# A turned bank of q and k that only ScalarE reads

## The chip, the core and the metric

The kernel runs on one core of one Trainium2 chip. What counts is the device time of one execution in microseconds (us). The names of the engines are those of the profile: PE is TensorE, DVE VectorE, ACT ScalarE, POOL GpSimd, SP SyncE; SBUF is the on-chip memory, PSUM the eight banks into which PE writes its products and its transposes.

## The reference

One layer of a hybrid decoder over 1024 tokens of width 1024, all in float32. An input projection feeds three head groups side by side: a gated short convolution, eight heads of stick-breaking attention, and a spatial gate; then an output projection, a squared-ReLU MLP, and an embedding with a gate. The part that this change touches is the QK norm and the scores:

```python
q = rms_norm(q.reshape(bsz, s_len, ATTN_HEADS, HEAD_DIM), q_norm_g[i])
k = rms_norm(k.reshape(bsz, s_len, ATTN_HEADS, HEAD_DIM), k_norm_g[i])
...
z = jnp.einsum('bqhd,bkhd->bhqk', qi, kj) * scale
log_rem = jnp.where(causal, jax.nn.log_sigmoid(-z), 0.0)
suffix = lax.cumsum(log_rem, axis=3, reverse=True) - log_rem
weights = jnp.where(causal, jnp.exp(log_beta + suffix), 0.0)
```

## The kernel before

**Two parts for each number.** PE multiplies in a rounded format (fp32r). Each operand is therefore kept as a hi part (the value rounded by ScalarE as it copies) and a lo part (the value less its hi part, made by VectorE), and a product is three matmuls: hi by hi, hi by lo, lo by hi. `split` (L130 to L139) makes such a pair: ScalarE writes hi, VectorE subtracts.

**Stages.** First the projection of the embedding and the norm of x, then the gate's and the first pair's projections, then attention, then the output projection, the MLP (products by a Strassen-like scheme, L814), the last gate. The attention stage runs from about 85 to 410 us. It weaves two streams: `attention()` goes through four pairs of heads (`pr`), and `fill` carries the projections of the pairs 1 to 3 (`project`, L340) and then the convolution. `weave` (L284) takes pieces from both so that PE has projection matmuls to do while the attention of the pair before waits for other engines. The order in which instructions stand in each engine's queue is set when the kernel is built, by a scheduler that plays the program on a model of time; a changed instruction can thus move its neighbours.

**The projection of a pair.** For each block of 128 tokens, `project` collects q, k and v of two heads in a PSUM bank (`qkv_ps`). ScalarE squares q and k (L376), VectorE sums (`ss`, L379), GpSimd takes the power -1/2 (`rs`, L170), VectorE writes q and k times `rs` to the SBUF tile `qk` (L384; one tile holds two blocks, and there are two such tiles). ScalarE and VectorE make v's parts (`V`, L137 and L138), and only then the bank `qkv_ps` is free for the next block.

**The turn.** After two blocks, `turn_qk` (L394) lets PE transpose the tile: four transposes go into one bank, `qk_tr`, q of both blocks in columns 0 to 255 and k in 256 to 511. There are 16 such turns, four for each pair of heads. Of the bank, ScalarE writes q's hi part to `QS` (L137) and k's to `KH` (L407); VectorE makes q's lo part `low_q` (L138, `q_lo` in the profile) and, for each of the two heads, k's lo part on that head's 64 rows (`KL`, L409, twice). After every second turn, copies bring the two heads' rows to their places (L413 to L418). The framework that places the semaphores lets only one engine at a time at a PSUM bank, readers included. So the bank changes hands: ScalarE (QS), VectorE (q_lo), ScalarE (KH), VectorE (KL, KL).

**Attention.** `stick` multiplies QS by KH and KL (`z`, L448 and L450), ScalarE takes the sigmoid (`rem`, L452), VectorE scans backwards (L457), and the weights are differences of neighbours (`wt`, L464), on VectorE for three of eight row blocks, on GpSimd for the rest. `gather` transposes the weights (`w_tr`, L486), splits them (`wT_hi`, `wT_lo`), and multiplies by V (`av`, L504). The banks of `qk_tr` and `w_tr` come from one pool of three (`ps_tr`): as long as one of the three is not read out, the other two have to do.

Of the kernel before, what the change touches and what calls it, by code (L numbers as in the profile page):

```python
# [10 lines left out]
AF = mybir.ActivationFunctionType  # L11
ALU = mybir.AluOpType
# [21 lines left out]
def hybrid_block(ctx: ExitStack, tc: tile.TileContext, a: dict):  # L34
# [5 lines left out]
    nc = tc.nc  # L40
# [42 lines left out]
    def bank(pool, s):  # L83
        return pool.tile([P, HT], F32, tag=pool.name, name=name(s))
# [30 lines left out]
    def load_const(key, shape):  # L115
        t = const.tile(list(shape), F32, name=f"c_{key}")
        nc.gpsimd.dma_start(t, a[key])
        return t
# [6 lines left out]
    gq = load_const("gq", [P, 1])  # L125
# [5 lines left out]
    def split(src, hi, lo, scale=None, low=nc.vector):  # L131

        if scale is None:
            last_hi[0] = nc.scalar.copy(hi, src)  # L134
            low.tensor_tensor(out=lo, in0=src, in1=hi, op=ALU.subtract)  # L135
        else:
            nc.scalar.activation(hi, src, AF.Copy, scale=scale)  # L137
            nc.vector.scalar_tensor_tensor(out=lo, in0=src, scalar=scale, in1=hi,  # L138
                                           op0=ALU.mult, op1=ALU.subtract)  # L139
# [205 lines left out]
    def project(pr):  # L345
# [11 lines left out]
        for t in range(KT):  # L357
# [34 lines left out]
            if t % 2 == 1:  # L392
                later(72, lambda t=t, qk=qk: turn_qk(heads[pr], t, qk))

    def turn_qk(head, t, qk):

        QS, KH, KL, _, low_q = head
        th = t // 4
        tr = bank(ps_tr, "qk_tr")
        for i in range(2):  # L400
            for j in range(2):
                o = j * 256 + i * P
                nc.tensor.transpose(tr[:, o:o + P], qk[:, i, j * P:(j + 1) * P], ident)
        ws = slice((t % 4 - 1) * P, (t % 4 + 1) * P)

        split(tr[:, :256], QS[0][th][:, ws], low_q[th][:, ws], scale=gq)
        nc.scalar.activation(KH[0][th][:, ws], tr[:, 256:], AF.Copy, scale=gk)  # L407
        for hh, own in enumerate((lo_p, hi_p)):
            nc.vector.scalar_tensor_tensor(out=KL[hh][th][own, ws], in0=tr[own, 256:],  # L409
                                           scalar=gk[own], in1=KH[0][th][own, ws],  # L410
                                           op0=ALU.mult, op1=ALU.subtract)
        if t % 4 == 3:
            nc.scalar.copy(KH[1][th][hi_p], KH[0][th][hi_p])  # L413
            nc.scalar.copy(KH[1][th][lo_p], KH[0][th][hi_p])
            nc.scalar.copy(KH[0][th][hi_p], KH[0][th][lo_p])
            nc.vector.tensor_copy(QS[1][th][hi_p], QS[0][th][hi_p])
            nc.vector.tensor_copy(QS[1][th][lo_p], low_q[th][hi_p])
            nc.vector.tensor_copy(QS[0][th][hi_p], low_q[th][lo_p])  # L418
        return 8
# [331 lines left out]
    def late_slot(tag, s, dt=F32):  # L751
        return late.tile([P, HT], dt, tag=tag, name=name(s), bufs=LATE[tag])
# [172 lines left out]
    for h in range(2):  # L925
        for n in (0, 4, 1, 5, 2, 6, 3, 7):
# [28 lines left out]
            t = hg[n][h] = late_slot("tmp", "hg")  # L955
# [151 lines left out]
    def residual(n, h):  # L1107
        if h_res[n][h] is None:
            h_res[n][h] = slot("h")
            nc.sync.dma_start(h_res[n][h], h_dram[n, h])  # L1110
        return h_res[n][h]
# [28 lines left out]
    for s, (c, p, j) in enumerate(steps):  # L1140
# [13 lines left out]
        elif p == 6:  # L1154
            subtract(nc.vector, u_sum[j], u_sum[j], bank)
            if last:
                add(nc.vector, h_res[j][1], h_res[j][1], u_sum[j])
                for h in range(2):
                    t = residual(j + 4, h)
                    subtract(nc.vector, t, t, u_sum[j])  # L1160
        elif p in (2, 3):
            t = residual(j, p - 2)
# [3 lines left out]
        else:  # L1166
            h = 0 if p == 4 else 1
            t = residual(j + 4, h)
# [55 lines left out]
    for p in GATE:  # L1224
        for j in range(4):
# [14 lines left out]
            for bank, c in zip(banks, cs):  # L1240
# [8 lines left out]
                elif p == 5:  # L1249
                    e_of[j] = late_slot("tmp", "e")  # L1250
                    add(nc.vector, e_of[j], bank, v_of[j])
                    t = late_slot("tmp", "gt")
                    add(nc.vector, t, d_bank.pop((3, j))[0], e_of[j])
                    gated(j, 1, t, t, c, by_dma=True)
                elif p == 7:
                    t = e_of[j][:, c]
                    add(nc.vector, t, bank, t)
                    gated(j + 4, 1, t, t, c, -1.0, True)
                elif p == 4:
                    t = v_of[j][:, c]  # L1260
# [84 lines left out]
```

## Time and profile before

| | |
|---|---|
| median of 3 runs | 1207.3 us (1204.84 to 1210.0) |
| the profiled execution, its own time | 1206.75 us |
| its span, first to last instruction | 1205.0 us |
| PE busy | 1181.0 us, 98% |
| DVE busy | 885.7 us, 73% |
| ACT busy | 595.5 us, 49% |
| POOL busy | 400.5 us, 33% |
| granted PE clock | 0.997 |

The page of the profile first gives busy times by engine. Its chain of waits goes back from the last instruction to what released each step. The view of waits tells, for each engine, which instruction stood idle and what ended it. The table by stretches gives the busy time of each engine in a part of the span, so that PE's idle time can be laid to a stage. The view of groups gives the number of instructions of one line and shape and the mean duration of one.

### The profile page before, as it was taken

Reading aid. Unit: us, or ns where it says so; the run is one execution under the profiler, and the core shown is the slowest. Engines: PE = TensorE matmul, PEld = TensorE weight load, DVE = VectorE, ACT = ScalarE, POOL = GpSimd, SP = SyncE. Lnnn points to the kernel's source line nnn. Section 1 sums busy time; section 2 is a strip of 40 time slices with the busy share of each in tenths; the row PEclk is TensorE's granted clock in tenths of the full one; section 3 lists DMA queues with packets and bytes.
Section 4 is the critical chain, followed back from the end, with each engine's and each line's share of the span. In section 5 each row is a group of like instructions: output and inputs, shape, how many; then the busy total and the mean of one; then the engine's idle time right before and its main releaser. Section 6 shows DMA issues by size and latency. Waiting matters only on the chain.

```text
span 1205.0 us, 17538 instructions
## 1 busy us (share of the span) xinstructions
PE 1181.0 (98%) x5788; PEld 1007.1 (84%) x5788; DVE 885.7 (73%) x1310; ACT 595.5 (49%) x1148; POOL 400.5 (33%) x472
## 2 busy tenths in 40 slices
PE   9999899998999999999999999999999999999997
PEld 7899899898888888888888888888888888888886
DVE  7846898989896667868877777787664657753697
ACT  7735565565643466733334333356543444456642
POOL 3324355464352222045354453421023301013412
PEclk9999999999999999999999999999999999999999
DMA  9602359999673776679998989777889975644857
GB/s 311 233 18 90 130 172 262 253 194 167 140 146 95 196 263 204 204 207 261 265 240 249 264 238 260 221 257 277 300 267 295 290 249 175 231 146 119 181 155 209
DMA packets 127963, 254.03 MB, mean 211 GB/s; under 512 B 14496, under 2 KB 22432, under 8 KB 127168
## 3 DMA queue, kind: packets, MB, share of 16 engines
q1 hardware_dynamic: 94992, 168.08, 41.4%
q0 software_dynamic: 27664, 57.05, 25.2%
q10 hardware_dynamic: 5216, 27.79, 6.4%
q8 instruction: 45, 0.74, 0.3%
q14 instruction: 46, 0.38, 0.1%
HBM read 192.30 MB, written 92.80 MB: 237 GB/s over the span
## 4 chain that ended last, share of the span: by engine, by line
PE 88%; DVE 8%; ACT 1%; issue 1%; DMA 1%; POOL 1%; SPq 0%; DVEq 0%; ACTq 0%; POOLq 0%
PE f_ps L814 25%; PE d_ps L814 25%; PE g_ps L814 6%; DVE rem L457 3%; PE qkv_ps L161 3%; PE qkv_ps L162 2%; PE qkv_ps L163 2%; PE o_ps L161 2%; PE o_ps L163 2%; PE o_ps L162 2%; PE av L504 2%; PE cv_ps L163 2%; PE cv_ps L161 2%; PE cv_ps L162 2%; PE w_tr L486 1%; PE vu_ps L162 1%
## 5 line engine op out<-in xcount | busy, mean ns | idle before, releaser
L135 DVE TENSOR_TENSOR w_lo<-raw,w_hi 128x512 fp32r<-128x512 f32 x280 | 243.1, 872 | 85.0 <-ACT w_hi L134 83.1
L134 ACT CAST w_hi<-raw 128x512 fp32r<-128x512 f32 x280 | 172.5, 620 | 240.5 <-PE d_ps L814 115.4
L814 PE MATMUL f_ps<-hn_hi,w_hi 128*128 128x512 f32 x448 | 175.2, 392 | 0.0
L814 PE MATMUL f_ps<-hn_lo,w_hi 128*128 128x512 f32 x448 | 174.9, 390 | 0.0
L814 PE MATMUL d_ps<-f_hi,w_hi 128*128 128x512 f32 x448 | 174.8, 390 | 0.0
L814 PE MATMUL f_ps<-hn_hi,w_lo 128*128 128x512 f32 x448 | 174.6, 391 | 0.0
L814 PE MATMUL d_ps<-f_hi,w_lo 128*128 128x512 f32 x448 | 174.3, 389 | 0.0
L814 PE MATMUL d_ps<-f_lo,w_hi 128*128 128x512 f32 x448 | 174.3, 389 | 0.0
L457 DVE TENSOR_TENSOR_SCAN rem<-rem,after 128x128 f32<-128x128 f32 (+3 forms) x64 | 90.9, 1431 | 13.3 <-ACT rem L452 13.3
L814 PEld LDWEIGHTS f_ps<-hn_lo,w_hi 128*128 128x128 f32 x448 | 84.5, 189 | 17.9 <-issue 0.2
L814 PEld LDWEIGHTS f_ps<-hn_hi,w_hi 128*128 128x128 f32 x448 | 84.5, 189 | 17.8 <-issue 0.2
L814 PEld LDWEIGHTS f_ps<-hn_hi,w_lo 128*128 128x128 f32 x448 | 84.5, 189 | 17.6
L814 PEld LDWEIGHTS d_ps<-f_hi,w_hi 128*128 128x128 f32 x448 | 84.1, 188 | 17.7 <-issue 0.2
L814 PEld LDWEIGHTS d_ps<-f_hi,w_lo 128*128 128x128 f32 x448 | 84.1, 188 | 17.6
L814 PEld LDWEIGHTS d_ps<-f_lo,w_hi 128*128 128x128 f32 x448 | 84.1, 188 | 17.5 <-issue 0.2
L161 PE MATMUL qkv_ps<-whi,xn_hi 128*128 128x384 f32 x256 | 88.8, 347 | 0.9 <-DVE V L138 0.8
L162 PE MATMUL qkv_ps<-wlo,xn_hi 128*128 128x384 f32 x256 | 86.6, 338 | 0.0
L163 PE MATMUL qkv_ps<-whi,xn_lo 128*128 128x384 f32 x256 | 86.3, 337 | 0.0
L135 DVE TENSOR_TENSOR f_lo<-raw,f_hi 128x512 fp32r<-128x512 f32 x112 | 78.2, 728 | 8.5 <-ACT f_hi L134 8.2
L134 ACT CAST f_hi<-raw 128x512 fp32r<-128x512 f32 x112 | 67.1, 620 | 25.6 <-DMA raw<-f_dram 21.6
L800 POOL TENSOR_TENSOR S<-S,sq 128x512 f32<-128x512 f32 x19 | 25.6, 1347 | 160.1 <-ACT sq L876 160.1
L452 ACT ACTIVATE rem<-z 128x128 f32<-128x128 f32 (+3 forms) x96 | 46.7, 500 | 24.3 <-PE z L450 21.6
(250 smaller groups left out, 2618.9 us busy)
## 6 DMA issues: line engine op xcount, KB each, us to landing
raw<-in_w_ff SPq DMA_DIRECT2D x148, 256.0 KB, 4.2
raw<-f_dram SPq DMA_DIRECT2D x112, 256.0 KB, 5.1
raw<-w_sums SPq DMA_DIRECT2D x64, 256.0 KB, 4.1
f_dram<-f SPq DMA_DIRECT2D x48, 256.0 KB, 3.9
f_dram<-t SPq DMA_DIRECT2D x48, 256.0 KB, 4.0
w_sums<-in_w_ff POOLq DMA_DIRECT2D x8, 1024.0 KB, 12.1
w_sums<-w_sums POOLq DMA_DIRECT2D x8, 1024.0 KB, 15.3
raw<-in_w_out SPq DMA_DIRECT2D x28, 256.0 KB, 3.5
```

Of the source, the lines that this page charges most:

```text
L134: last_hi[0] = nc.scalar.copy(hi, src)
L135: low.tensor_tensor(out=lo, in0=src, in1=hi, op=ALU.subtract)
L161: nc.tensor.matmul(ps, lh, rh, start=first and i == 0, stop=False)
L162: nc.tensor.matmul(ps, lh, rl, start=False, stop=False)
L163: done = nc.tensor.matmul(ps, ll, rh, start=False, stop=last and i == len(terms) - 1)
L452: last_act[0] = nc.scalar.activation(rem[:, ks], z, AF.Sigmoid, scale=-HD ** -0.5)
L457: nc.vector.tensor_tensor_scan(out=back, data0=back, data1=after[:, T - W:][:, ::-1], initial=1.0, op0=ALU.mult, op1=ALU.max)
L486: nc.tensor.transpose(tr[:, n:n + P], wts[i][:, kb * P:(kb + 1) * P], ident)
L504: nc.tensor.matmul(av[:, first * P:], lhs, part[:, o:o + m], start=kb == 0 and part is hi, stop=kb == 2 * g + 1 and part is lo)
L800: return eng.tensor_tensor(out=out, in0=x, in1=y, op=ALU.add)
L814: done = nc.tensor.matmul(bank, l, r, start=first and k == 0 and i == 0, stop=k == len(b) - 1 and i == 2, skip_group_check=True)
```

## The change

In `turn_qk`, ScalarE now reads the bank three times in a row: QS, KH, and a plain copy of all 512 columns, written over the tile `qk` that was just transposed (its rows seen as 512 columns, `turned`). VectorE no longer touches the bank: q_lo and both KL are made from `turned`, in SBUF, by the same operation with the same scalar and second input.

```diff
-        split(tr[:, :256], QS[0][th][:, ws], low_q[th][:, ws], scale=gq)
+
+        nc.scalar.activation(QS[0][th][:, ws], tr[:, :256], AF.Copy, scale=gq)
         nc.scalar.activation(KH[0][th][:, ws], tr[:, 256:], AF.Copy, scale=gk)
+        turned = qk.rearrange("p t c -> p (t c)")
+        nc.scalar.copy(turned, tr)
+        nc.vector.scalar_tensor_tensor(out=low_q[th][:, ws], in0=turned[:, :256], scalar=gq,
+                                       in1=QS[0][th][:, ws], op0=ALU.mult, op1=ALU.subtract)
         for hh, own in enumerate((lo_p, hi_p)):
-            nc.vector.scalar_tensor_tensor(out=KL[hh][th][own, ws], in0=tr[own, 256:],
+            nc.vector.scalar_tensor_tensor(out=KL[hh][th][own, ws], in0=turned[own, 256:],
                                            scalar=gk[own], in1=KH[0][th][own, ws],
                                            op0=ALU.mult, op1=ALU.subtract)
```

In the changed kernel all lines from here on stand five numbers higher (L464 is L469 there); q_lo is L411, KL is L414, and the scaled hi parts are L407 and L408, the copy L410. The scheduler also moves other instructions of the attention stage; outside it the order is as before. Three places on VectorE matter here (the number behind a name tells tiles of one name apart).

First, the third turn of a pair of heads, beside the long rows of attention (here pair 1's attention with pair 2's projection; in the profile before, this is the place at 209 to 217 us). Before:

```order
L457 SCALAR_TENSOR_TENSOR rem_2467<-rem_2467,after 128x1024
L379 TENSOR_REDUCE ss_2644<-qk_sq_2641 128x4
L138 SCALAR_TENSOR_TENSOR q_lo_2263<-qk_tr_2534,c_gq,QS_2262 128x256
L464 TENSOR_TENSOR wt_2468<-rem_2467 128x1023
L457 SCALAR_TENSOR_TENSOR rem_2569<-rem_2569,after 128x896
L409 SCALAR_TENSOR_TENSOR KL_2257<-qk_tr_2534,c_gk,KH_2261 64x256
L409 SCALAR_TENSOR_TENSOR KL_2259<-qk_tr_2534,c_gk,KH_2261 64x256
```

With the change:

```order
L462 SCALAR_TENSOR_TENSOR rem_2475<-rem_2475,after 128x1024
L379 TENSOR_REDUCE ss_2653<-qk_sq_2650 128x4
L469 TENSOR_TENSOR wt_2476<-rem_2475 128x1023
L411 SCALAR_TENSOR_TENSOR q_lo_2270<-qk_2372,c_gq,QS_2269 128x256
L414 SCALAR_TENSOR_TENSOR KL_2264<-qk_2372,c_gk,KH_2268 64x256
L414 SCALAR_TENSOR_TENSOR KL_2266<-qk_2372,c_gk,KH_2268 64x256
L462 SCALAR_TENSOR_TENSOR rem_2578<-rem_2578,after 128x896
```

The three lo parts now stand together, behind the difference `wt` and ahead of the scan of 896; before, the two KL stood behind that scan. In the same place of pair 0's attention KL and `wt` are moved in a like way, save that q_lo and one KL stay ahead of `wt`.

Second, VectorE at the fourth turn, where the copies L416 to L418 follow (pair 0's attention; 159 to 165 us in the profile before). Before:

```order
L138 SCALAR_TENSOR_TENSOR q_lo_1410<-qk_tr_1882,c_gq,QS_1409 128x256
L384 TENSOR_TENSOR qk_1914<-qkv_ps_1797,rs_1912 128x256
L135 TENSOR_TENSOR wT_lo_1879<-w_tr_1873,wT_hi_1878 128x512
L409 SCALAR_TENSOR_TENSOR KL_1404<-qk_tr_1882,c_gk,KH_1408 64x256
L409 SCALAR_TENSOR_TENSOR KL_1406<-qk_tr_1882,c_gk,KH_1408 64x256
L416 COPY QS_1411<-QS_1409 64x512
L417 COPY QS_1411<-q_lo_1410 64x512
L138 SCALAR_TENSOR_TENSOR V_1916<-qkv_ps_1797,r_731,V_1916 128x2x64
L418 COPY QS_1409<-q_lo_1410 64x512
```

With the change:

```order
L135 TENSOR_TENSOR wT_lo_1884<-w_tr_1878,wT_hi_1883 128x512
L384 TENSOR_TENSOR qk_1920<-qkv_ps_1802,rs_1918 128x256
L421 COPY QS_1415<-QS_1413 64x512
L411 SCALAR_TENSOR_TENSOR q_lo_1414<-qk_1709,c_gq,QS_1413 128x256
L414 SCALAR_TENSOR_TENSOR KL_1408<-qk_1709,c_gk,KH_1412 64x256
L414 SCALAR_TENSOR_TENSOR KL_1410<-qk_1709,c_gk,KH_1412 64x256
L422 COPY QS_1415<-q_lo_1414 64x512
L423 COPY QS_1413<-q_lo_1414 64x512
L138 SCALAR_TENSOR_TENSOR V_1922<-qkv_ps_1802,r_731,V_1922 128x2x64
```

Behind `qk` stood wT_lo, KL, KL and two copies ahead of V; now q_lo, KL, KL and three copies stand there, and wT_lo has gone ahead of `qk`.

Third, VectorE in pair 1's attention, beside the first blocks of pair 2's projection (185 to 190 us in the profile before). Before:

```order
L457 SCALAR_TENSOR_TENSOR rem_2292<-rem_2292,after 128x384
L457 SCALAR_TENSOR_TENSOR rem_2307<-rem_2307,after 128x512
L464 TENSOR_TENSOR wt_2308<-rem_2307 128x511
L384 TENSOR_TENSOR qk_2110<-qkv_ps_2115,rs_2204 128x256
L379 TENSOR_REDUCE ss_2360<-qk_sq_2357 128x4
```

With the change:

```order
L462 SCALAR_TENSOR_TENSOR rem_2300<-rem_2300,after 128x384
L462 SCALAR_TENSOR_TENSOR rem_2315<-rem_2315,after 128x512
L384 TENSOR_TENSOR qk_2117<-qkv_ps_2122,rs_2211 128x256
L469 TENSOR_TENSOR wt_2316<-rem_2315 128x511
L138 SCALAR_TENSOR_TENSOR V_2119<-qkv_ps_2122,r_731,V_2119 128x2x64
```

`qk`, for which the next turn's transposes wait, has gone ahead of `wt`.

## The prediction

> **What bounds the kernel.** I read the page's busy times first, then its chain, then the table by stretches.
>
> ```profile
> PE 1181.0 (98%) x5788; PEld 1007.1 (84%) x5788; DVE 885.7 (73%) x1310; ACT 595.5 (49%) x1148; POOL 400.5 (33%) x472
> PE 88%; DVE 8%; ACT 1%; issue 1%; DMA 1%; POOL 1%; SPq 0%; DVEq 0%; ACTq 0%; POOLq 0%
> ```
>
> PE is busy but for 24 us of the 1205.0 us span, and 88% of the chain is PE: PE bounds the kernel, and a change that leaves PE's work alone can at best take PE's idle time. The turns lie between 85 and 326 us. The table by stretches (start and end; length, then busy PE, PEld, DVE, ACT, POOL; clock; DMA) shows how much there is:
>
> ```profile
> 105.00:130.00 25.00, 23.24 (x144) 22.77 (x144) 18.75 (x37) 15.89 (x42) 14.58 (x19) 1.00 0.43 148
> 130.00:165.00 35.00, 31.69 (x199) 28.91 (x197) 30.81 (x38) 17.07 (x41) 11.54 (x14) 1.00 0.37 128
> 165.00:190.00 25.00, 23.42 (x161) 22.68 (x161) 23.97 (x39) 16.31 (x44) 19.59 (x30) 1.00 0.89 238
> 190.00:232.00 42.00, 39.86 (x251) 37.16 (x250) 37.12 (x52) 23.17 (x56) 19.04 (x23) 1.00 0.93 246
> 232.00:278.00 46.00, 45.12 (x294) 43.19 (x294) 39.43 (x64) 29.37 (x76) 29.00 (x44) 1.00 0.87 191
> 278.00:310.00 32.00, 29.05 (x192) 27.21 (x193) 30.21 (x46) 18.26 (x45) 13.60 (x18) 1.00 0.79 148
> 505.00:1110.00 605.00, 605.00 (x2680) 500.76 (x2679) 416.85 (x561) 270.01 (x461) 177.97 (x180) 1.00 0.79 241
> ```
>
> In the MLP (last row) PE never stops, so nothing can be won there. From 105 to 310 us PE idles 1.8 + 3.3 + 1.6 + 2.1 + 0.9 + 3.0 = 12.6 us, about 1% of the time. Beside it DVE is 88% busy (180.3 of 205 us): PE is fed by a DVE that is almost full. The view of waits names what ended these idle times (first four rows, 85 to 330 us) and who else waited at the bank:
>
> ```profile
> PE w_tr L486 <- DVE KL L409: 3.6, 4, 1.5
> PE w_tr L486 <- DVE wt L464: 3.2, 3, 1.6
> PE av L504 <- DVE wT_lo L135: 2.9, 4, 1.8
> PE qk_tr L403 <- DVE qk L384: 1.5, 1, 1.5
> ACT KH L407 <- DVE q_lo L138: 9.0, 10, 3.7
> DVE KL L409 <- ACT KH L407: 1.1, 2, 0.5
> DVE q_lo L138 <- ACT QS L137: 0.5, 1, 0.5
> ```
>
> The hand-over of the bank is to be seen: the transposes w_tr wait 3.6 us for KL to leave a bank that they want, and ScalarE waits 9.0 us for q_lo only to read other columns of it.
>
> **What is added.** The rows of the groups (busy us, mean ns of one | idle before):
>
> ```profile
> L590 ACT COPY y_c<-c_tr 128x512 f32<-128x512 f32 x4 | 2.3, 586 | 0.8 <-PE c_tr L588 0.8
> L138 DVE SCALAR_TENSOR_TENSOR q_lo<-qk_tr,c_gq,QS 128x256 fp32r<-128x256 f32 x16 | 7.5, 471 | 0.6 <-ACT QS L137 0.5
> L409 DVE SCALAR_TENSOR_TENSOR KL<-qk_tr,c_gk,KH 64x256 fp32r<-64x256 f32 x32 | 15.3, 479 | 1.5 <-ACT KH L407 1.1
> L384 DVE TENSOR_TENSOR qk<-qkv_ps,rs 128x256 f32<-128x256 f32 x32 | 13.3, 416 | 10.1 <-POOL rs L170 9.9
> L135 DVE TENSOR_TENSOR wlo<-stage,whi 128x256 fp32r<-128x256 f32 x8 | 3.3, 416 | 0.2 <-ACT whi L134 0.2
> ```
>
> The copy is of the form of y_c: 16 x 0.586 = 9.4 us more on ScalarE. It is busy 104.2 of 180 us between 130 and 310 us (58%), and the 9.0 us that it stood before KH go. So I price the copies at nothing; without that cover, were half of ScalarE's 9.4 us on the path, it would be +4.7 us.
>
> **What is moved.** 48 DVE operations (16 q_lo, 32 KL; 22.8 us) change a PSUM input for an SBUF one. By the last two rows a 128x256 subtraction or product takes 416 ns from either, so the operations themselves cost the same: 0. But with the change both inputs lie in SBUF, and such operations have a second price. Three instructions (start, duration), and two groups of 128x384 in the stretch 85 to 330 us, the first with both inputs in SBUF, the second with one in PSUM:
>
> ```profile
> 288.78 1.25 POOL L464 TENSOR_TENSOR wt<-rem 128x639 f32<-128x639 f32 x1
> 289.08 2.03 DVE L464 TENSOR_TENSOR wt<-rem 128x1023 f32<-128x1023 f32 x1
> 212.20 1.21 DVE L464 TENSOR_TENSOR wt<-rem 128x1023 f32<-128x1023 f32 x1
> L135 DVE TENSOR_TENSOR wlo<-stage,whi 128x384 fp32r<-128x384 f32 x19 | 18.1, 963 | 0.0
> L135 DVE TENSOR_TENSOR wT_lo<-w_tr,wT_hi 128x384 fp32r<-128x384 f32 x25 | 13.7, 548 | 1.0 <-ACT wT_hi L134 0.8
> ```
>
> The same difference of 1023 takes 1.21 us at 212 us, and 2.03 us at 289 us, where GpSimd had begun one 0.3 us earlier: VectorE stood until GpSimd was done. In the groups this makes 963 against 548 ns, 0.415 us for an operation. The Trainium skill has the rule (State Buffer, section "Who interferes with whom"): a VectorE instruction with two SBUF inputs contends with a GpSimd instruction that reads SBUF, and whoever is first holds the shared port to its end. The trace agrees, 2.03 against 1.21 us, and it speaks against this change; without it the sum below would be -1.1 instead of -0.6 us.
>
> Bounds on DVE: 0 and 48 x 0.415 = 19.9 us. The upper one is too high, as the wlo stand where GpSimd makes wlo too, and of three operations in a row only the first finds GpSimd already at work. Where were the worst places? At the third turn:
>
> ```profile
> 213.33 2.01 DVE L457 TENSOR_TENSOR_SCAN rem<-rem,after 128x896 f32<-128x896 f32 x1
> 215.26 0.96 DVE L409 SCALAR_TENSOR_TENSOR KL<-qk_tr,c_gk,KH 64x256 fp32r<-64x256 f32 x2
> 215.48 1.68 POOL L464 TENSOR_TENSOR wt<-rem 128x895 f32<-128x895 f32 x1 [1.32 <-DVE rem L457]
> 216.36 0.63 PE L486 MATMUL w_tr<-ident,wt 128*128 128x128 f32 x4 [0.86 <-DVE KL L409]
> ```
>
> GpSimd's difference of 895 follows the scan of 896 by its data, and the second KL would have met it. With the changed order the KL stand ahead of that scan, and miss it. I take +0.5 us on the path, between 0 and 10 (half of 19.9, since some half of the turns lie where PE waits for DVE), near the lower end for this reason.
>
> **What is removed: 3.6 us of PE idle, of which little counts.** In the rows above, the bank is late by the scan (2.01 us) that DVE does first. With the change ScalarE frees it. Then PE goes on at once, but to projection matmuls, and stops at the next thing that DVE has to give. After three of the four KL waits (3.6 - 1.5 = 2.1 us together) that is V, which frees qkv_ps. The place at the fourth turn:
>
> ```profile
> 162.90 0.97 DVE L409 SCALAR_TENSOR_TENSOR KL<-qk_tr,c_gk,KH 64x256 fp32r<-64x256 f32 x2
> 164.70 0.35 DVE L138 SCALAR_TENSOR_TENSOR V<-qkv_ps,r,V 128x128 fp32r<-128x128 f32 x1
> 165.08 0.42 DVE L418 CAST QS<-q_lo 64x512 fp32r<-64x512 f32 x1
> 165.11 0.44 PE L161 MATMUL qkv_ps<-whi,xn_hi 128*128 128x384 f32 x1 [0.34 <-DVE V L138]
> ```
>
> DVE works without a pause up to it, so the 2.1 us only make the wait for V longer: 0 won. What is late next is V itself: in the changed order the third copy (0.42 us) stands ahead of V. At 165 us q_lo (0.47) comes in behind `qk` and wT_lo of 512 (0.68) goes out, +0.2; at 232 us the set is the same but for the copy, +0.4. Together +0.6 us.
>
> The fourth KL wait (1.5 us at 282.8 us) is followed by waits in a chain that ScalarE leads:
>
> ```profile
> 293.22 0.47 ACT L137 ACTIVATE QS<-qk_tr,c_gq 128x256 fp32r<-128x256 f32 x1
> 294.85 0.48 ACT L407 ACTIVATE KH<-qk_tr,c_gk 128x256 fp32r<-128x256 f32 x1 [1.15 <-DVE q_lo L138]
> 295.22 0.58 ACT L134 CAST wT_hi<-w_tr 128x512 fp32r<-128x512 f32 x1
> ```
>
> Done in a row, QS, KH and the copy end at 293.22 + 0.47 + 0.48 + 0.59 = 294.76, against 295.33: -0.6 us.
>
> **What the new order gives.** The wait of PE at 189 us, 1.5 us in the view of waits:
>
> ```profile
> 187.54 1.13 DVE L464 TENSOR_TENSOR wt<-rem 128x511 f32<-128x511 f32 x1
> 188.59 0.41 DVE L384 TENSOR_TENSOR qk<-qkv_ps,rs 128x256 f32<-128x256 f32 x1
> 189.06 0.44 PE L403 MATMUL qk_tr<-ident,qk 128*128 128x128 f32 x2 [1.47 <-DVE qk L384]
> ```
>
> With `qk` ahead of `wt` that wait shrinks by wt's 1.13 us, and PE has no gap from there to 213 us: -1.1 us (bounds -1.5 and 0, if GpSimd's rs is late). The first scores also move up on PE, by one block of projection; PE's wait of 1.8 us at 121 us is for a wT_lo that stands behind as much DVE work as before, so I take 0 there (bounds -1.8 and 0).
>
> The sum: 0 + 0.5 + 0.6 - 0.6 - 1.1 = -0.6 us. On the profiled execution's own 1206.75 us (span 1205.0) that is 1206.15; the median of the runs shown lies 0.55 us above that execution, so the forecast is 1206.7 us.
>
> **Rivals.** First, the waits vanish and do not come back: DVE is only 88% full, so its work may move up too. Then the KL waits (3.6), the first wait (1.8), the one at 189 us (1.1) and the ScalarE chain (0.6) all count: -7.1, 1207.3 - 7.1 = 1200.2 us. For it: ScalarE loses 9.0 us of standing, and the bank pool has three banks instead of two. Against it: the row of 164.70, where V ends an unbroken run of DVE work. Second, slower by one mechanism: the lo parts queue behind GpSimd's differences and weight parts. At 0.415 us for all 48, half on the path, it is +10; with V's +0.6, 1217.9 us. It decides from about 6 us, that is some 15 operations on the path that meet GpSimd at work. For it: the groups of 963 and 548 ns; against it: the order, as said. Third, the change does not do what it says: the copy comes last of the three, on an engine with other work queued, so that the bank may be free no sooner than by KL before. Then nothing is won, the waits stay where they are: 1207.3 us.
>
> **How the numbers follow.** About 0.5%, 6 us, is what a measurement of this kernel can tell from no change. Forecast (1204 to 1209 us): 0.50. Vanishing waits (around 1200): 0.24. GpSimd (1212 and up): 0.14. No effect: 0.12. Of the vanishing waits I put 0.20 below 1201.3 us, and 0.02 of the forecast: faster 0.22. Of GpSimd 0.13 is above 1213.3 us, and 0.02 of the forecast: slower 0.15. The rest, 0.63, is within 0.5%. The likeliest case's own range is 1204 to 1209; the range that holds 8 in 10 runs from the vanishing waits' 1200 to 1213, where the bound on GpSimd is cut at half.
>
> **What would show it.** Right: no wait of w_tr for KL and none of KH for q_lo; a wait for V at the fourth turns longer by what KL's were; the wait at 189 us nearly gone; q_lo and KL at 0.47 to 0.5 us but for a few. Wrong: PE's idle time from 105 to 310 us below 7 us (first rival), or means of q_lo and KL above 0.7 us and PE idle above 18 us (second).

## The result: 0.36% slower

The changed kernel took 1212.85 us (median of 18 runs, 1209.78 to 1214.77) beside 1207.45 us for the kernel before in the same comparison (18 runs, 1204.84 to 1211.24): a ratio of 1.0036, 95% interval 1.0026 to 1.0045. That lies within 0.5% and inside the wide range (1200 to 1213 us), but above the likeliest case's own range (1204 to 1209 us) and on the other side of no change from the sum: -0.6 us was forecast, about +4.3 us came. The profiled execution of the changed kernel took 1214.03 us, 7.3 us more than that of before, at a granted clock of 0.995 against 0.997.

The page of the changed kernel, busy times and the chain by engine:

```profile
PE 1184.8 (98%) x5788; PEld 1009.2 (83%) x5788; DVE 898.0 (74%) x1310; ACT 599.4 (49%) x1164; POOL 397.9 (33%) x472
PE 87%; DVE 8%; DMA 2%; ACT 1%; issue 1%; POOL 1%; SPq 0%; ACTq 0%; DVEq 0%; POOLq 0%
```

The table by stretches of the changed kernel (start and end; length, then busy PE, PEld, DVE, ACT, POOL; clock; DMA):

```profile
105.00:130.00 25.00, 23.17 (x135) 22.73 (x135) 18.45 (x35) 15.90 (x40) 13.18 (x18) 0.93 0.45 148
130.00:165.00 35.00, 31.58 (x193) 29.01 (x192) 29.57 (x32) 16.43 (x41) 11.93 (x15) 1.00 0.38 128
165.00:190.00 25.00, 23.60 (x164) 22.88 (x163) 23.15 (x40) 17.45 (x46) 15.87 (x24) 1.00 0.64 164
190.00:232.00 42.00, 39.09 (x246) 36.06 (x245) 37.03 (x49) 24.37 (x60) 24.21 (x28) 1.00 1.07 282
232.00:278.00 46.00, 44.54 (x290) 42.79 (x289) 39.70 (x66) 27.57 (x72) 25.69 (x39) 1.00 0.87 193
278.00:310.00 32.00, 28.86 (x182) 25.75 (x181) 30.11 (x41) 18.39 (x44) 14.94 (x20) 1.00 0.82 148
505.00:1110.00 605.00, 605.00 (x2679) 500.72 (x2678) 428.87 (x566) 269.82 (x463) 173.30 (x176) 1.00 0.80 242
```

The MLP is as full as it was. From 105 to 310 us PE now idles 1.8 + 3.4 + 1.4 + 2.9 + 1.5 + 3.1 = 14.1 us, against 12.6, and in the first stretch it runs at a clock of 0.93. More is added behind the last turn, from 330 to 430 us, where PE idles 2.6 us against 0.7 (first before, then changed):

```profile
330.00:430.00 100.00, 99.30 (x511) 83.12 (x510) 74.57 (x99) 42.40 (x84) 33.29 (x39) 1.00 0.66 162
330.00:430.00 100.00, 97.42 (x507) 81.11 (x506) 77.48 (x103) 41.91 (x84) 32.38 (x41) 1.00 0.64 146
```

The view of waits, 85 to 330 us:

```profile
PE qkv_ps L161 <- DVE V L138: 7.1, 7, 1.8
ACT KH L420 <- DVE KL L414: 3.5, 3, 1.3
DVE q_lo L411 <- ACT qk L410: 2.2, 4, 0.9
PE av L509 <- DVE wT_lo L135: 1.9, 4, 0.7
PE w_tr L491 <- DVE wt L469: 1.9, 3, 0.9
PE av L509 <- ACT y_both L518: 1.3, 2, 0.8
PE z L453 <- ACT rem L457: 1.1, 2, 0.7
PE qk_tr L403 <- DVE qk L384: 0.5, 1, 0.5
```

The change did what it says: no w_tr waits for KL (3.6 us before) and no KH for q_lo (9.0 us). In their place PE waits 7.1 us for V (0.8 before), and VectorE stands 2.2 us until the copy (L410) is done (before: 0.5 us for QS and 1.1 us for KH). The lo parts became longer, 0.534 and 0.542 us against 0.479 and 0.471:

```profile
L414 DVE SCALAR_TENSOR_TENSOR KL<-qk,c_gk,KH 64x256 fp32r<-64x256 f32 x32 | 17.1, 534 | 0.2
L411 DVE SCALAR_TENSOR_TENSOR q_lo<-qk,c_gq,QS 128x256 fp32r<-128x256 f32 x16 | 8.7, 542 | 2.6 <-ACT qk L410 2.2
```

One place shows both. The timeline at the second turn (start, duration, engine, instruction, in brackets the idle time before):

```profile
113.27 2.61 POOL L135 TENSOR_TENSOR wlo<-stage,whi 128x384 fp32r<-128x384 f32 x2
113.78 1.24 DVE L411 SCALAR_TENSOR_TENSOR q_lo<-qk,c_gq,QS 128x256 fp32r<-128x256 f32 x1
114.94 2.36 DVE L414 SCALAR_TENSOR_TENSOR KL<-qk,c_gk,KH 64x256 fp32r<-64x256 f32 x2
115.91 1.10 POOL L135 TENSOR_TENSOR wlo<-stage,whi 128x384 fp32r<-128x384 f32 x1
117.33 0.35 DVE L138 SCALAR_TENSOR_TENSOR V<-qkv_ps,r,V 128x128 fp32r<-128x128 f32 x1
117.74 0.44 PE L161 MATMUL qkv_ps<-whi,xn_hi 128*128 128x384 f32 x1 [1.83 <-DVE V L138]
```

GpSimd makes three weight parts (wlo) from 113.3 to 117.0 us, and each of VectorE's three lo parts is held by one of them: 1.24 + 2.36 = 3.60 us for what takes 1.44 us elsewhere. V is late by the difference, and PE pauses 1.83 us. In a run below with the same order, whose lo parts read the bank (psum_in_after), PE does not pause from 105 to 130 us at all:

```profile
105.00:130.00 25.00, 25.00 (x157) 24.61 (x156) 19.65 (x40) 18.19 (x46) 14.89 (x19) 1.00 0.45 148
```

### The profile page after: what moved, and what is told of

Read it like the earlier page. It is cut to its first block, busy times and chain, and to the rows that moved or that the text cites. A ratio compares the mean times of both kernels' runs of the same rounds, so it can differ in the third digit from the quotient of the medians.

```text
span 1212.3 us, 17554 instructions
## 1 busy us (share of the span) xinstructions
PE 1184.8 (98%) x5788; PEld 1009.2 (83%) x5788; DVE 898.0 (74%) x1310; ACT 599.4 (49%) x1164; POOL 397.9 (33%) x472
## 4 chain that ended last, share of the span: by engine, by line
PE 87%; DVE 8%; DMA 2%; ACT 1%; issue 1%; POOL 1%; SPq 0%; ACTq 0%; DVEq 0%; POOLq 0%
PE f_ps L819 25%; PE d_ps L819 25%; PE g_ps L819 6%; PE qkv_ps L161 3%; PE qkv_ps L163 3%; PE qkv_ps L162 3%; PE o_ps L161 2%; PE o_ps L163 2%; PE o_ps L162 2%; DVE rem L462 2%; PE av L509 2%; PE w_tr L491 1%; PE vu_ps L162 1%; PE vu_ps L161 1%; PE vu_ps L163 1%
## 5 line engine op out<-in xcount | busy, mean ns | idle before, releaser
L135 DVE TENSOR_TENSOR w_lo<-raw,w_hi 128x512 fp32r<-128x512 f32 x280 | 248.8, 893 | 85.2 <-ACT w_hi L134 83.2
L170 POOL TENSOR_TENSOR rs<-ss,mhalf 128x4 f32<-128x4 f32 x32 | 40.5, 1266 | 61.4 <-DVE ss L379 61.4
```

The lines of the kernel that those rows point to most:

```text
L170: last_power[0] = nc.gpsimd.tensor_tensor(out=out, in0=in_, in1=mhalf[:, :n], op=ALU.pow)
```

## What the experiments are compared by

The time of one and the same program varies with the granted clock of PE. In 131 executions of the kernel before, beside the experiments, those at a mean clock of 0.993 (11) took 1211.3 us on average, those at 0.998 (17) 1206.7 us: 0.92 us for each thousandth. So beside the ratio each table gives the mean of time times clock, that is, about what the program would take at full clock. For the kernel before it was 1203.7, 1203.8, 1203.8, 1203.7 and 1203.8 us in five comparisons. (A thousandth of clock moves this product by 1.2 us, more than the 0.92 us measured; where two clocks differ much, I give both readings.) The product is known to within some 0.4 to 1.3 us (two standard errors), by the number of runs.

## First experiments: one suspected cause each

Three theories. Port: the second SBUF input makes the lo parts meet GpSimd. Order: the scheduler's new order puts KL ahead of the third turn's scan of 896, so that the scan of 1024 meets GpSimd. ScalarE: 16 copies more delay its other work.

**hi_first**: before, with ScalarE's two reads in a row, no copy.

```diff
-        split(tr[:, :256], QS[0][th][:, ws], low_q[th][:, ws], scale=gq)
+        nc.scalar.activation(QS[0][th][:, ws], tr[:, :256], AF.Copy, scale=gq)
         nc.scalar.activation(KH[0][th][:, ws], tr[:, 256:], AF.Copy, scale=gk)
+        nc.vector.scalar_tensor_tensor(out=low_q[th][:, ws], in0=tr[:, :256], scalar=gq,
+                                       in1=QS[0][th][:, ws], op0=ALU.mult, op1=ALU.subtract)
```

> The kernel before with one thing of the change: ScalarE makes QS and KH in a row, then VectorE makes q_lo, KL, KL, all from the PSUM bank; no copy. Port theory (the lo parts are slow because both their inputs lie in SBUF): these have one SBUF input, so q_lo and KL at 0.47 and 0.48 us each, and a time within 1 us of before. Order theory (the scheduler's new order, with both KL ahead of the scan of 896 at the third turn, lets the scan of 1024 meet GpSimd's difference of 895): this kernel's order has the KL there too, so the second scan of 1024 at 3.2 us or more at the third turns (2.5 to 2.8 before) and 2 to 4 us slower than before. ScalarE theory (the 16 copies delay ScalarE's other work): as before or up to 1 us faster.

**after_psum**: the changed kernel, with the copy, but the lo parts read the bank.

```diff
-        ...in0=turned[:, :256], scalar=gq,
+        ...in0=tr[:, :256], scalar=gq,
-        ...in0=turned[own, 256:],
+        ...in0=tr[own, 256:],
```

> The changed kernel with its copy, but VectorE makes q_lo and KL from the PSUM bank after the copy; the copy's result is not used. Port theory: most of the loss goes, ratio to before below 1.0015. Order theory: the KL still stand ahead of the scan of 896, so the loss stays, ratio 1.002 to 1.004, with scans of 1024 at 3.2 us or more. ScalarE theory: the loss stays, 1.003 to 1.005.

**kl_ahead**: before, with the third turn's scan of 896 issued behind KL.

```diff
+                    if hh == 1 and t == 6 and pr < 3:
+                        order.enter_context(tc.issue_after(last_kl[0].ins))
                     nc.vector.tensor_tensor_scan(out=back, data0=back,
```

> The kernel before, with its own instructions and its own PSUM reads; only that the second scan of 896 of the pairs 0 to 2 is issued on VectorE behind the KL of the third turn (the scheduler then moves some neighbours). Order theory: second scan of 1024 at 3.2 us or more at the third turns, PE's waits for KL gone or moved to V, and 1.5 to 4 us slower than before (ratio 1.001 to 1.0035). Port theory and ScalarE theory: the same time as before, ratio 0.999 to 1.001.

**act_load**: before, with a useless copy on ScalarE in each turn.

```diff
         nc.scalar.activation(KH[0][th][:, ws], tr[:, 256:], AF.Copy, scale=gk)
+        turned = qk.rearrange("p t c -> p (t c)")
+        nc.scalar.copy(turned, turned)
```

> The kernel before, and on ScalarE one more copy of 128x512 for each turn, from SBUF onto itself (its result is not used): the load of the change's copies without its hand-over and without its SBUF reads on VectorE; the order at the third turns is that of before. ScalarE theory: 3 to 5 us slower, ratio 1.0025 to 1.004. Order and port theories: ratio 0.999 to 1.0012.

| | ratio to before, 95% interval | mean clock | time x clock, us |
|---|---|---|---|
| before | 1 | 0.9952 to 0.9961 | 1203.8 |
| changed | 1.0036 (1.0026 to 1.0045) | 0.9959 | 1207.7 |
| hi_first | 0.9982 (0.9971 to 0.9993) | 0.9958 | 1201.6 |
| after_psum | 1.0030 (1.0019 to 1.0041) | 0.9943 | 1205.6 |
| kl_ahead | 0.9998 (0.9987 to 1.0009) | 0.9962 | 1204.3 |
| act_load | 0.9982 (0.9971 to 0.9993) | 0.9967 | 1202.7 |

Read as they stand, all three theories fall: after_psum has no second SBUF input (its KL are back at 0.479 us) and loses as much; kl_ahead has the meeting at the scan (its scans of 1024 at 219 and 286 us take 3.37 and 3.70 us, against 2.46 and 2.81 in the kernel before) and loses nothing; act_load has ScalarE's load and gains. But act_load cannot have gained by a useless copy. The scheduler had put the other engines' work in another order for it, and so for each of these kernels. No two of them differ by their edit alone.

## The same order for different operations

So I held the order. The instructions of these kernels are the same but for the copy, and can be matched one by one, engine by engine. A list of their numbers, taken from the built program of one kernel, then links each instruction of another to the one before it on its engine, in issue order only:

```diff
+ORDER = {"PE": "91-98 ...", "DVE": "...", "Activation": "...", "Pool": "...", "SP": "..."}
+        for one, then in zip(names, names[1:]):
+            tc.add_manual_dep(traced[then], one, link, reason="in_order")
...
         hybrid_block(tc, a)
+        in_order(tc)
```

In the names below, `X_in_Y` is the operations of X in the order of Y. KH, and the copy where there is one, follow QS directly (in the order of before and act_load that is the one thing moved; `before_in_act` keeps KH where it was).

> The changed kernel's operations, with every engine's instructions held in the order in which they stand in the kernel of hi_first (each copy directly behind its KH). Theory Order (the time is set by the order that comes out for the engines, whatever the operations): as hi_first, 0.998 of before, 1205 us. Theory Operations (the copies, the longer chain QS, KH, copy ahead of the lo parts, and their SBUF inputs cost the time in any order): 1.003 to 1.004, 1211.5 us. In between means that both have a share.

> The operations of hi_first (QS and KH in a row, then the lo parts from PSUM, no copy), with every engine's instructions held in the order of the changed kernel. Order: as the changed kernel, 1.0036 of before, 1212 us. Operations: as hi_first, 0.998, 1205 us.

> The changed kernel's operations in the order of before, but for KH and the copy, which follow QS directly. Order: 1.000 of before. Operations: 1.003 or more, since before's order was made for lo parts that come sooner.

> The operations of hi_first in the order of before, but for KH, which follows QS directly. Order: 1.000 of before. Operations: 0.998, since ScalarE no longer stands 9.0 us before KH and nothing is added.

The next four take the changed kernel's operations apart. `psum` is after_psum (copy, lo parts from the bank). `load` is hi_first with ScalarE's useless copy behind KH. `port` is hi_first with the lo parts made from another SBUF tile, so that they are not those of the reference:

```diff
-        ...low_q[th][:, ws], in0=tr[:, :256], scalar=gq,
+        ...low_q[th][:, ws], in0=xn[0][0][0].bitcast(F32)[:, :256], scalar=gq,
```

> The changed kernel with the lo parts read from the PSUM bank, not from the copy (but still waiting for the copy, which reads the same bank ahead of them), held in hi_first's order. In that order hi_first took 0.998 of before, and the changed kernel's operations 1.004. Theory Delay (VectorE stands for the third ScalarE operation, 4 us in all, and what is queued behind slips): 1.002 to 1.004, with q_lo's standing at 5 us as in after_in_hi. Theory Port (the second SBUF input, 3.5 us of longer lo parts): 0.998. Theory Load (ScalarE's 9.4 us): 1.004.

> hi_first in its own order, but the lo parts' first input is the left half of an early tile of xn in SBUF instead of the turned bank, so that they are computed from other data and the output is not the reference's. It has the second SBUF input and no copy, and the bank is freed by ScalarE. Port: 1.002 to 1.004, with means of q_lo and KL at 0.53 to 0.59 us. Delay and Load: 0.998.

> hi_first in its own order, with ScalarE copying the tile of qk onto itself behind each KH (0.62 us, 16 times); the lo parts don't wait for it. Load: 1.003 or more. Delay and Port: 0.998 to 0.999.

> The kernel before, unchanged in its operations, in the order that came out for act_load (which has the copy of qk onto itself and took 0.998 of before). If an order alone is worth 0.2%: 0.998. If act_load gained by something else: 1.000.

Then the same operations in the orders that were still missing, and two runs with lo parts that read one SBUF input (`one_input`, the subtraction of the hi part left out):

```diff
-        nc.vector.scalar_tensor_tensor(out=low_q[th][:, ws], in0=turned[:, :256], scalar=gq,
-                                       in1=QS[0][th][:, ws], op0=ALU.mult, op1=ALU.subtract)
+        nc.vector.tensor_scalar(out=low_q[th][:, ws], in0=turned[:, :256][:, ::-1], scalar1=gq,
+                                scalar2=0.5, op0=ALU.mult, op1=ALU.subtract)
```

> The changed kernel with the lo parts read from the PSUM bank (and waiting for the copy), in the order of before (KH and copy behind QS). In that order the changed kernel's operations took 1.0039 of before, with a mean of 0.75 us for KL, and hi_first's operations 0.9995. Port: 0.9995 to 1.001. Delay: 1.003 or more.

> The same operations as in psum_in_before, in the changed kernel's own order. The bank is then held until the lo parts have read it, as in hi_in_after (1.0036), where PE waited 10.7 us for KL in an order made for a bank that comes free sooner. Port alone: between 0.999 and 1.002. If the order, made for an early bank, costs by itself without the copies' tile: 1.003 to 1.005, as hi_in_after, with PE waiting for KL by some 10 us.

> The changed kernel's operations in a fourth order, that of act_load (KH and copy behind QS), in which the kernel before took 0.9975. If the operations cost some 0.4% to 0.6% in whatever order: 1.002 to 1.004. If an order can hide them: 0.998.

> hi_first's operations in act_load's order (KH behind QS): the control for after_in_act, and a candidate that beats both kernels. If operations and order add: 0.997 to 0.998, and after_in_act above it by 0.4% to 0.6%.

> The changed kernel in its own order, with the copy, its delay and the early bank all as they are, but q_lo and KL made by a one-input instruction (copy times scale, less 0.5, read backwards) instead of by the two-input one; the subtraction of the hi part is left out, so the output is not the reference's. If contention is what costs the changed kernel its time in its own order too: 1.000 or less, with lo parts of even length (0.4 to 0.5 us, no longer ones). If it is not: 1.003 to 1.004.

> The same one-input lo parts in hi_first's order, where the changed kernel took 1.0040 and the variant that reads PSUM 0.9996. Contention: 0.998 to 0.9996. Otherwise: 1.003 to 1.004.

| operations in order of | ratio to before, 95% interval | mean clock | time x clock, us |
|---|---|---|---|
| hi_in_before | 0.9995 (0.9983 to 1.0007) | 0.9965 | 1203.7 |
| psum_in_before | 1.0000 (0.9991 to 1.0010) | 0.9965 | 1205.2 |
| after_in_before | 1.0039 (1.0026 to 1.0052) | 0.9948 | 1207.4 |
| hi_first (own) | 0.9982 (0.9971 to 0.9993) | 0.9958 | 1201.6 |
| load_in_hi | 0.9990 (0.9979 to 1.0001) | 0.9954 | 1201.8 |
| psum_in_hi | 0.9996 (0.9984 to 1.0008) | 0.9958 | 1203.1 |
| port_in_hi | 1.0016 (1.0004 to 1.0028) | 0.9945 | 1204.1 |
| one_input_in_hi | 1.0009 (0.9998 to 1.0019) | 0.9942 | 1202.6 |
| after_in_hi | 1.0040 (1.0027 to 1.0054) | 0.9932 | 1205.6 |
| hi_in_after | 1.0036 (1.0022 to 1.0049) | 0.9913 | 1202.8 |
| psum_in_after | 1.0030 (1.0019 to 1.0041) | 0.9930 | 1204.4 |
| one_input_in_after | 1.0016 (1.0004 to 1.0028) | 0.9956 | 1205.3 |
| changed (own) | 1.0036 (1.0026 to 1.0045) | 0.9959 | 1207.7 |
| before_in_act | 0.9975 (0.9963 to 0.9987) | 0.9961 | 1202.0 |
| hi_in_act | 1.0019 (1.0009 to 1.0029) | 0.9939 | 1204.5 |
| after_in_act | 1.0066 (1.0054 to 1.0078) | 0.9932 | 1208.9 |

**By the last column the changed operations cost about 4 us more than hi_first's in each of four orders**: 3.7 (before), 4.0 (hi_first), 4.9 (its own) and 4.4 us (act_load). By time alone they cost 0.44, 0.58 and 0.47% in the first, second and fourth of these orders, and nothing in their own (1.0036 both), where hi_first's operations run at the lowest clock of all (0.9913; the section on the hardware shows why). So the cost is of the operations, but in the changed kernel's own order it shows only at equal clock. It has two parts:

- *The copy ahead of the lo parts* (psum less hi): 1.5, 1.5 and 1.6 us, each known to 0.8 to 1.4 us; by time alone it is +0.05, +0.14 and -0.06%, too little to tell from nothing. It is not ScalarE's load, since a copy that nobody waits for costs 0.2 us (load less hi_first, within the error). It is VectorE, which stands until the third operation is done: 4.7 us for q_lo in psum_in_hi, where hi_first had 1.2 (first hi_first, then psum_in_hi):

```profile
DVE q_lo L408 <- ACT KH L407: 1.2, 4, 0.5
DVE q_lo L411 <- ACT qk L410: 4.7, 8, 0.9
```

- *Reading the copy in SBUF* (changed less psum): 2.2, 2.5 and 3.3 us; by itself, without any copy (port less hi_first), 2.5 us. By time alone it is +0.39, +0.44 and +0.06%, and +0.34% for port. In this difference the bank that comes free sooner is already counted, so the contention alone may cost more.

With 0.92 us for a thousandth of clock in place of 1.2, the changed operations cost 4.2, 4.8, 3.5 and 4.6 us more than hi_first's, the copy 1.5, 1.5 and 1.1, and reading it 2.7, 3.3 and 2.4 us: much the same.

In the order of before the lo parts meet GpSimd far more often than in the changed kernel's own. The groups of after_in_before and of psum_in_before, 84 to 335 us, the first fence after_in_before:

```profile
L414 DVE SCALAR_TENSOR_TENSOR KL<-qk,c_gk,KH 64x256 fp32r<-64x256 f32 x32 | 24.0, 751 | 0.2
```

```profile
L414 DVE SCALAR_TENSOR_TENSOR KL<-qk_tr,c_gk,KH 64x256 fp32r<-64x256 f32 x32 | 15.3, 477 | 0.2
```

In these two the operations and the order are the same but for the input, and the waits of PE show where the early bank goes. First after_in_before, then psum_in_before:

```profile
PE qkv_ps L161 <- DVE V L138: 10.0, 6, 2.5
```

```profile
PE w_tr L491 <- DVE KL L414: 3.7, 4, 1.5
PE qkv_ps L161 <- DVE V L138: 1.6, 3, 0.7
```

The 3.7 us for KL vanish, and 8.4 us are added for V: VectorE works the same list, 8.7 us of KL longer, and PE meets it at its next product.

The one-input runs did not take the contention away, as they were meant to. Their KL (one_input_in_after, all 32: shortest, median, longest in ns) are shorter, but the longest are held as before:

```profile
L414 DVE TENSOR_SCALAR KL<-qk,c_gk x32: 336/353/1160, 94.9 to 325.8; 64x256 fp32r<-64x256 f32 x32
```

What they tell is another thing: 48 lo parts that are 5.9 us shorter in all (13.3 + 6.6 against 17.1 + 8.7 us), with bank, copy and order unchanged, give 2.4 us back. So some 40% of VectorE's time at the lo parts is on the path there; in hi_first's order it was 3.0 us of 5.9 (13.3 + 7.3 against 17.1 + 9.4).

## Why the prediction failed

The forecast in the changed kernel's own order can now be taken step by step, by time times clock: before 1203.8; hi_first's operations in that order 1202.8 (-1.0); with the copy ahead of the lo parts 1204.4 (+1.6); with the lo parts read from the copy and the bank free early 1207.7 (+3.3). Each step is uncertain by about 1.3 us where psum_in_after is in it. With 0.92 us for a thousandth of clock, they are +0.3, +1.1 and +2.4 us. By time alone they are +4.4, -0.7 and +0.7 us, since the two kernels in the middle lose the most clock. The other way round, operations first and order last, the time needs no clock beside it: in the order of before 0.9995 with hi_first's operations, 1.0000 with the copy ahead, 1.0039 with the copy read, and then 1.0036 in the new order. There too it is reading the copy that costs.

- **"So I price the copies at nothing": failed, some +1.1 to 1.6 us instead of 0 at equal clock.** The cover that it named, ScalarE's free time, was there (0.2 us in load_in_hi). The price was looked for on the wrong engine. The lo parts wait for the copy; the prediction counted three ScalarE operations in a row and never asked what VectorE does meanwhile. It stands 2.2 us for the copy, where hi_first's operations in the same order stood 0.4 us, with V and wT_lo queued behind.
- **Contention, "+0.5 us on the path": failed, some 2.2 to 3.3 us, with what the early bank won already taken off.** Its mechanism was right, its bounds held, and the place it looked at was right too: at the third turn the KL stand ahead of the scan and take 0.97 us for two at 216.67 us. But it took the third turn for the worst place of all. At 113.8 us, in the rows above, GpSimd's wlo hold all three lo parts, where it had said that of three in a row only the first finds GpSimd at work. In all the lo parts are 2.9 us longer, 2.2 us of them at that one turn. A price near zero for a resource that two engines share wanted a look at every turn, not at one kind.
- **The KL waits become waits for V: right.** In one order (the changed kernel's), PE waited 10.6 us for KL with the lo parts read from the bank and none with the copy; V went from 0.9 to 7.1 us, and the sum of all PE waits from 13.0 to 13.8 us. Freeing the bank won nothing that VectorE did not take back.
- **V behind the third copy, +0.6 us: right in kind.** The fourth turn at 165 us of the changed kernel:

```profile
167.34 0.42 DVE L422 CAST QS<-q_lo 64x512 fp32r<-64x512 f32 x1
167.79 0.42 DVE L423 CAST QS<-q_lo 64x512 fp32r<-64x512 f32 x1
168.24 0.35 DVE L138 SCALAR_TENSOR_TENSOR V<-qkv_ps,r,V 128x128 fp32r<-128x128 f32 x1
168.65 0.44 PE L161 MATMUL qkv_ps<-whi,xn_hi 128*128 128x384 f32 x1 [1.40 <-DVE V L138]
```

  That wait grew from 0.34 to 1.40 us. At the third turns V stands behind the scan of 896 that the KL had passed, which the prediction did not follow (1.34 us at 220.00).
- **`qk` ahead of `wt`, -1.1 us: right at that wait, half of it given back.** PE's pause there was 1.47 us and is 0.47, but at 192.70 us it now pauses 0.51 us for V, where the kernel before had no gap:

```profile
191.75 0.44 PE L403 MATMUL qk_tr<-ident,qk 128*128 128x128 f32 x2 [0.47 <-DVE qk L384]
192.70 0.41 PE L161 MATMUL qkv_ps<-whi,xn_hi 128*128 128x384 f32 x1 [0.51 <-DVE V L138]
```

- **First scores, 0: the number came, by luck.** The first long pause was 1.76 us for wT_lo and is 1.83 us for V. The wait for wT_lo was forecast to stay, and it did not: in the new order with the lo parts read from the bank PE does not pause there (the row of psum_in_after above). The new order took the wait away, and the contention put another in its place. The ScalarE chain at 293 us (-0.6 us) can't be told from its neighbours: from 278 to 310 us PE idles 3.1 us against 2.9.
- **The rivals.** Vanishing waits did not come (1200.2 us): the sum of all PE waits from 85 to 330 us did not fall. GpSimd's contention at 1217.9 us had one of the two causes, at three to five times its size. That nothing happens is out: the waits moved as forecast.

That the other terms also add up to about -1 us (0.6 - 0.6 - 1.1), like the step of the order, confirms nothing: that step is measured with hi_first's operations, with which PE waits 10.7 us for KL. What failed is two terms of the same kind, time of VectorE that the change adds at the lo parts: 0.5 us in the sum, about 4.9 us at equal clock (3.5 with 0.92 us for a thousandth). A third thing stands in no term: the forecast followed the new order only as far as the turns. Behind them, from 330 to 430 us, PE idles 1.8 to 2.6 us in the four kernels that stand in this order, whatever their operations, against 0.7 to 1.4 in the four in the order of before.

**What stays open.** In the changed kernel's own order the split of 4.9 us into 1.6 and 3.3 rests on seven runs of psum_in_after and is known to 1.3 us; the clock is on record only for the changed kernel's 18 runs, not for those of before beside them. The lo parts are only 2.9 us longer in all there, and the idle time of PE from 84 to 430 us differs by 1.7 us between the profiles of psum_in_after and of the changed kernel, so how the whole 2.4 to 3.3 us comes about is not shown. What the early bank alone is worth was not isolated: nothing that was tried frees the bank early and leaves VectorE out of GpSimd's way. Why before's operations gain 1.8 us in act_load's order (1202.0), and hi_first's lose 0.8 us there, was not followed.

## What the runs showed of the hardware

**A pause of PE can cost half a clock for 3.4 us more.** hi_in_after has the lowest clock of all (0.9913) although its product is below that of before: by time it loses 0.36%, by time times clock it gains 1.0 us. Its profile shows why. PE's pause at 148 us, and the stretches around it (the column before the last two is the clock):

```profile
148.00 0.30 PE L488 MATMUL w_tr<-ident,wt 128*128 128x128 f32 x1 [3.65 <-DVE KL L411]
```

```profile
146.00:148.00 2.00, 0.00 (x0) 0.03 (x1) 1.94 (x4) 0.00 (x0) 0.00 (x0) 1.00 0.00 0
148.00:150.00 2.00, 2.00 (x8) 1.23 (x8) 1.97 (x2) 1.02 (x2) 0.00 (x0) 0.68 0.00 0
150.00:152.00 2.00, 2.00 (x11) 2.00 (x12) 2.00 (x3) 1.51 (x4) 1.68 (x1) 0.50 0.00 0
152.00:154.00 2.00, 2.00 (x13) 1.92 (x13) 2.00 (x2) 1.44 (x4) 0.00 (x0) 0.97 0.00 0
```

From 0.7 us after the pause's end PE runs at half clock for 3.4 us (2 x 0.32 + 2 x 0.50 + 2 x 0.03 = 1.7 us lost). I went through the 20 profiles of this study between 84 and 430 us, pauses from PE's timeline, clock in stretches of 2 us. Of 30 pauses of 1.2 to 1.75 us none was followed by such a stretch; of 34 from 1.76 to 3.65 us 22 were (one of them for 6.8 us), among them two of the four of 2.48 us and all six longer ones; and in this part of the span no such stretch came without a pause of that length before it. Elsewhere it did: in 8 of the 20 profiles, that of before among them, 3.4 us at half clock lie between 514 and 528 us, where PE is busy without a break, beginning at the end of a group of products of two columns (ms_ps, 128x2) or within 2 us of it. Why is not shown. The Trainium skill (TensorE: Matmul & The Clock Gate, HAM oscillation — how this bites in real kernels) gives the rule as no idle gaps above about 3.4 us. The traces here do not agree with that bound: 20 of the 22 followed pauses between 1.76 and 3.37 us. So a wait of 1.9 us can be worth 3.6 us, and two waits of 1 us are worth 2. What decides between pauses of 1.8 to 2.5 us that do and don't bring it was not found.

This also bears on the first table. after_psum lost 0.30% by time, but about half of that was clock (0.9943): its product is 1.8 us above before's, and 2.1 below the changed kernel's.

**Contention holds one-input instructions too.** The KL with a single SBUF input took 353 ns at the median and up to 1160 when GpSimd was at its weight parts. So it is not the second input alone that makes VectorE wait, as I had it.

**An order is worth as much as a change.** The kernel before, with no operation changed, took 0.9975 (0.9963 to 0.9987) of its time in the order that was made for act_load. That is the lowest ratio found, and beats both kernels, though the 0.9982 of hi_first and of act_load lie within its interval. hi_first, one line moved, has 0.9982 in the order made for it and 0.9995 in that of before, so most of its gain by time may be order too.

## What to carry to other kernels

An operation put between a producer and a full engine costs that engine's standing time, however idle the engine is that does it: price it where its result is waited for. Freeing a buffer early wins nothing if the engine that held it is the one that PE waits for next, and moving that engine's reads to SBUF beside a busy GpSimd made it slower here. Where a scheduler orders the work, an edit and its order are tested together; hold the order, and compare both the time and the time at equal clock, before a cause is believed or dropped.
